# Forgetting attention on one core: low parts of queries against high parts of keys alone, two key chunks at a time on the two halves of the array's rows

## The chip, the cores and the metric

The kernel runs on one core of one Trainium2 chip. The metric is the device time of one launch in microseconds (us). The kernel before took 3076.02 us, the median of three runs (3070.25 to 3080.53).

## The reference

The kernel computes one hybrid layer on 2048 tokens of width 1024 in float32: a norm, one combined input projection, three branches (forgetting attention, a state-space branch with a gated unit, attention into 256 memory tokens), a gated merge, an output projection and a last norm. The change is in the forgetting attention, 12 heads of 64 channels, causal, with a forget term F added to the scores:

```python
def forgetting_attention(q, k, v, log_f):
    F = jnp.cumsum(log_f, axis=1).transpose(0, 2, 1)
    ...
    def block(args):
        qi, Fi, s0 = args
        s = jnp.einsum('bhqd,bhkd->bhqk', qi, kh)
        s = s + Fi[..., None] - F[:, :, None, :]
        qpos = s0 + jnp.arange(Q_BLOCK, dtype=jnp.int32)
        s = jnp.where(key_pos[None, :] <= qpos[:, None], s, NEG)
        p = jax.nn.softmax(s, axis=-1)
        return jnp.einsum('bhqk,bhkd->bhqd', p, vh)
```

## The kernel before

**Numbers in two parts.** Matmuls take operands in a rounded float32 form (float32r). To keep float32 accuracy each operand is split into a high part and a low part, and a product is built from three matmuls: high by high, high by low, low by high (`mm3`, lines 147 to 149).

**Stages.** First come the norm, the transposes and the projections of the four token chunks, with the state-space branch, the gated unit and the memory attention threaded between the projections. Queries, keys and values go to scratch tensors in HBM in high and low parts (`s_qh`, `s_ql`, `s_kh`, `s_kl`, `s_vs`). Then comes the forgetting attention, from about 1605 to 2512 us of the span. A second generator, `fill`, threads the remaining gate projections (`gl`) and part of the merge between its steps, so that TensorE has other work while a softmax is under way. Last come the merge of the other chunks and the output projection.

**The forgetting attention.** `gen_fox` goes through the heads. A head's 16 blocks of 128 queries are taken in eight groups G of two blocks, from the last group to the first, and the short groups alternate with the next head's long ones. A head has 64 channels, and the array has 128 rows, so `fox_keys` (line 706) puts the high parts of 1024 keys in partitions 0 to 63 of the tile `kk` and the low parts in partitions 64 to 127. `fox_q` (line 719) loads the high parts of the queries twice, one copy over the other, as tile `qh`, and the low parts twice as tile `ql`.

`fox_scores` (line 730) takes one block of 128 queries against chunks of 512 keys. A block needs 1 to 4 chunks, by how far back its keys reach; the last chunk may have 128, 256, 384 or 512 keys, and at least 256 columns are computed. Each chunk has a PSUM bank of tag A and two matmuls: line 750 (`qh` with `kk`: high by high plus high by low) and line 751 (`ql` with `kk`: low by high plus low by low). VectorE then adds -F and takes the running maximum out of the bank (line 752), ScalarE takes the exponential (line 757), GpSimd scales the rows (line 761).

`fox_pv` (line 765) follows one group behind. For each two blocks of 128 keys, the rows are transposed by TensorE into a bank of tag B (line 782), ScalarE copies the high part (line 785, or 790 on the diagonal), VectorE takes the low part (line 786 or 791), and line 798 multiplies with the values into the one bank of tag C.

**What sets the order.** The program is built with a scheduler that places the instructions of all the threads in each engine's queue by its own model of time. The eight PSUM banks are divided by tag in the table `PS2` (line 43): A 3, B 3, C 1, F 1. The bank F and, in turn, A serve the threaded projections. All loads of keys and queries are issued by SyncE.

**A place with halves of the array.** The state-space branch already has matmuls that use half of the array, in columns: line 585 multiplies 64 columns of weights at a time into partitions 0 to 63 or 64 to 127 of its bank:

```python
for g in range(2):
    for ri in range(2):
        nc.tensor.matmul(pv[64 * g:64 * g + 64, ri * 256:(ri + 1) * 256],
                         m1t[:, ri * 128 + 64 * g:ri * 128 + 64 * g + 64], u[:, g, :], start=True, stop=True)
```

These are plain float32, and the profile has two records for each. Lines 550, 551 and 572 beside it are transposes and a small matmul of 16 columns.

Of the kernel before, what the change touches and what calls it, by code (L numbers as in the profile page):

```python
# [12 lines left out]
D = 1024  # L13
# [28 lines left out]
PSB = {"A": 2, "B": 3, "C": 2, "F": 1}  # L42
PS2 = {"A": 3, "B": 3, "C": 1, "F": 1}

# [5 lines left out]
class Layer:  # L50
# [83 lines left out]
    def load_w(self, src, shape, pool=None, bufs=2):  # L134
        """One [128, 1024] slab of weights, split into two float32r parts."""
        raw = self.wp.tile([128, 4 * NV], F32, tag="wraw", name="wraw", bufs=2)
        k, m = shape
        n = k * m
        self.nc.sync.dma_start(out=raw[:, :n], in_=src)
        hi, lo = ((pool or self.wp).tile([128, n if bufs == 1 else 1024], F32R, tag=t, name=t, bufs=bufs) for t in ("whi", "wlo"))  # L140
        self.split(hi[:, :n], lo[:, :n], raw[:, :n])
        return (hi[:, :n].rearrange("p (k m) -> p k m", k=k), lo[:, :n].rearrange("p (k m) -> p k m", k=k))

    def mm3(self, out, a, b, first, last):
        """a = (hi, lo) stationary, b = (hi, lo) moving."""
        nc = self.nc
        nc.tensor.matmul(out, a[0], b[0], start=first, stop=False)  # L147
        nc.tensor.matmul(out, a[0], b[1], start=False, stop=False)  # L148
        nc.tensor.matmul(out, a[1], b[0], start=False, stop=last)  # L149

    def rsqrt(self, p, out, ssq, n):
        """out = 1 / sqrt(ssq / D + eps): table square root, then a Newton step."""
        nc = self.nc
        v = p.tile([128, n], F32, tag="nv", name="nv", bufs=2)
        t = p.tile([128, n], F32, tag="nt", name="nt", bufs=2)
        nc.vector.tensor_scalar(out=v, in0=ssq, scalar1=1.0 / D, scalar2=EPS, op0=ALU.mult, op1=ALU.add)
        nc.scalar.activation(t, v, AF.Sqrt)
        nc.vector.reciprocal(out, t)
        nc.vector.tensor_mul(t, out, out)
        nc.vector.tensor_mul(t, t, v)  # L160
        nc.vector.tensor_scalar(out=t, in0=t, scalar1=-0.5, scalar2=1.5, op0=ALU.mult, op1=ALU.add)
        nc.vector.tensor_mul(out, out, t)

    def norm_T(self, src, nt, g, hi, lo, p, xb, split=False):
        """RMSNorm of nt tiles of 128 tokens, then transposed and split: hi, lo [128, KD, nt*128]."""
        nc = self.nc
# [23 lines left out]

# [1 line left out]
    def open_h(self):  # L192
# [63 lines left out]
    def proj_v(self, g, p):  # L256
        """Values of four heads; the forget gates ride with the first four."""
        nc, s = self.nc, self.s
# [29 lines left out]
    def forget(self, p):  # L288
        """-F, the running sum of -log sigmoid(z)."""
        nc, z = self.nc, self.fz  # L290
        e = p.tile([H, L], F32, name="fe")
        nc.vector.scalar_tensor_tensor(out=e, in0=z, scalar=-1.0, in1=z, op0=ALU.mult, op1=ALU.max)
        nc.scalar.activation(e, e, AF.Exp, scale=-1.0)
        nc.scalar.activation(e, e, AF.Ln, bias=1.0)
        nc.vector.scalar_tensor_tensor(out=z, in0=z, scalar=0.0, in1=e, op0=ALU.min, op1=ALU.subtract)
        one = p.tile([H, 1], F32, name="fo")
        nc.vector.memset(one, 1.0)
        nc.vector.tensor_tensor_scan(e, one.to_broadcast([H, L]), z, 0.0, ALU.mult, ALU.subtract)
        nc.sync.dma_start(out=self.s["nf"], in_=e)
# [106 lines left out]

# [1 line left out]
    def s5_exp(self, p, out, x):  # L408
        """exp(x): range reduction by ln 2, polynomial, exact power of two."""
        v = self.nc.vector  # L410
# [14 lines left out]
    def s5_reduce(self, t, n):  # L425
        """t - 2 pi round(t / 2 pi), in place."""
        v = self.nc.vector
# [5 lines left out]
    def s5_sincos(self, p, sn, cs, t, n):  # L433
        """sin and cos of t in [-pi, pi] (t is overwritten) by the quarter angle and two doublings."""
        v = self.nc.vector
# [16 lines left out]
    def cmul(self, outr, outi, ar, ai, br, bi, t):  # L452
        """(outr, outi) = (ar, ai) (br, bi); t is scratch; the outputs are none of the inputs."""
        v = self.nc.vector
# [7 lines left out]
    def s5_prep(self, q, p):  # L462
        """Discretised parameters in the layout [(group parity, state), group pair]; q keeps, p is scratch."""
        nc, v, i = self.nc, self.nc.vector, self.i
# [69 lines left out]
    def s5_pair(self, q, a):  # L534
        """Groups 2a and 2a+1. Chunks of 8 steps: what a chunk adds to the state (M1), the state at each chunk's
        end (a real scan of the states turned back by the phase they have run through), and the outputs from the
        state before the chunk (M2) and from the chunk's own inputs (M3)."""
        nc, v, s = self.nc, self.nc.vector, self.s
# [102 lines left out]

# [1 line left out]
    def mem_scores(self, p, hd, j, b, P):  # L643
# [56 lines left out]

# [1 line left out]
    def open_fox(self):  # L702
# [3 lines left out]
    def fox_keys(self, h, c):  # L706
        """Half a head's keys (high over low parts), values (high beside low) and -F."""
        nc, s, p = self.nc, self.s, self.fp
# [3 lines left out]
        nf = p.tile([128, 1024], F32, tag="nf", name="nf", bufs=3)  # L712
        nc.sync.dma_start(out=fl32(kk[0:64]), in_=s["kh"][r, ks])
        nc.sync.dma_start(out=fl32(kk[64:128]), in_=s["kl"][r, ks])
        nc.sync.dma_start(out=nf, in_=s["nf"][h:h + 1, ks].partition_broadcast(128))
# [14 lines left out]
    def fox_scores(self, p, hd, q, G, P):  # L730
        """Softmax rows of two blocks of 128 queries, the later one first: the mask goes into -F for good, as no
        later block of queries is left to read those keys unmasked."""
        nc = self.nc
        for b in (1, 0):
# [8 lines left out]
            mx = p.tile([128, 4], F32, tag="mx", name="mx", bufs=4)  # L743
            for c in range(nch):
                w = min(512, nk - c * 512)
                wm = max(w, 256)
                kk, _, nf = hd[c // 2]
                c0 = c % 2 * 512
                ps = self.psA()
                nc.tensor.matmul(ps[:, :wm], q[0][:, qs], kk[:, c0:c0 + wm], start=True, stop=False)  # L750
                nc.tensor.matmul(ps[:, :wm], q[1][:, qs], kk[:, c0:c0 + wm], start=False, stop=True)  # L751
                nc.vector.tensor_tensor_reduce(  # L752
                    out=pr[:, c * 512:c * 512 + w], in0=ps[:, :w], in1=nf[:, c0:c0 + w], scale=1.0,
                    scalar=-3.0e38, op0=ALU.add, op1=ALU.max, accum_out=mx[:, c:c + 1])
            nm, den, rd = (p.tile([128, 1], F32, tag=n, name=n, bufs=4) for n in ("nm", "den", "rd"))
# [9 lines left out]
    def fox_pv(self, p, h, hd, G, P):  # L765
        """Columns of the moving operand and of the sums: high parts of the two query blocks, then low parts."""
        nc, s = self.nc, self.s
# [41 lines left out]
    def gen_fox(self):  # L809
        """Heads one after the other, groups of queries from the last to the first; a head's last KS groups, the  # L810
        short ones, alternate with the next head's first ones."""
        p, self.close_f = self.pool("fox", side="right")
# [32 lines left out]

# [1 line left out]
    def gen_glu(self):  # L847
# [39 lines left out]
    def split(self, hi, lo, x, sc=1.0):  # L887
        """sc * x as hi + lo, each exact in float32r."""
        self.nc.gpsimd.tensor_scalar(out=hi, in0=x, scalar1=sc, scalar2=1.0, op0=ALU.mult, op1=ALU.mult)  # L889
# [7 lines left out]
    def ytile(self):  # L897
        """Slots of 4 KB, twelve in the first pool and ten in the second, in the order in which they come free."""
        i, self.ny = self.ny, self.ny + 1
# [20 lines left out]
    def gen_merge0(self):  # L920
        """The last chunk, under the last heads; its share of the attention as soon as the last head is past it."""
        nc, c = self.nc, NC - 1
# [129 lines left out]

# The channels of the state-space branch are kept, 128 at a time, in the order (channel of a group, group).
def host_arrays(x, mem, g_norm, g_mem_norm, g_final, w_in, b_forget, b_merge, w_mem_kv,
# [68 lines left out]
```

## Time and profile before

| | |
|---|---|
| median of three runs | 3076.02 us (3070.25 to 3080.53) |
| span of the profiled execution, first to last instruction | 3072.7 us |
| mean granted TensorE clock | 0.987 |
| PE (TensorE matmul) busy | 2995.7 us |
| DVE (VectorE) busy | 1884.8 us |
| ACT (ScalarE) busy | 927.8 us |
| POOL (GpSimd) busy | 1004.8 us |
| matmuls of lines 750 and 751 | 480 each |

PE is TensorE's matmuls, PEld its weight loads, SP is SyncE. A row of a group gives line, engine, operation, what is written and read, its shape as weights (rows*columns) and output (partitions x columns), the count, the busy time, the mean duration in ns, and then the idle time of the engine just before, with what ended it ("issue" where the profile shows no reason). Matmuls are pipelined: their durations overlap, so that the price of one is read from the distance between two starts. A row of the timeline gives the start, the length to the end of the last one merged into the row, and the count.

### The profile page before, as it was taken

The page shows a single profiled execution, that of the slowest core. Times are in us where ns is not written, and L with a number is a line of the kernel's source. Part 1 is how long each engine was busy: PE and PEld are TensorE (multiplying, and loading weights), DVE is VectorE, ACT ScalarE, POOL GpSimd, SP SyncE. Part 2 cuts the span into 40 slices and gives each one's busy share as a digit, 9 for nine tenths or more (in the row PEclk, how much of TensorE's full clock was granted, in tenths as well). Part 3 has the DMA queues.
Part 4 walks back from the last instruction along what each step waited for, and adds up shares of the span by engine and source line. Part 5 has one row for each costly group of instructions (what it writes and reads, how often), then busy time and mean ns, then how long its engine had stood idle before and what let it go on. Part 6 is the DMA issues. An engine that isn't in the chain of part 4 may idle for free.

```text
span 3072.7 us, 43527 instructions
## 1 busy us (share of the span) xinstructions
PE 2995.7 (97%) x14656; PEld 2438.1 (79%) x14656; DVE 1884.8 (61%) x4982; ACT 927.8 (30%) x1881; POOL 1004.8 (33%) x1328
## 2 busy tenths in 40 slices
PE   9999999999999999999999999999999998999999
PEld 7889977777777778888878888888887786777787
DVE  5333489888886673322217777777777886555544
ACT  5102111111112231222216666666666550000011
POOL 0010000000001332121205665655555766555500
PEclk9999999999999999999999999999999998999999
DMA  5343323323344655344352443544434536665531
GB/s 167 107 136 96 105 84 116 115 84 111 114 132 150 175 164 173 108 127 136 115 165 82 124 121 103 134 121 121 118 111 130 145 108 195 185 182 172 159 108 69
DMA packets 283118, 396.81 MB, mean 129 GB/s; under 512 B 83060, under 2 KB 147828, under 8 KB 282884
## 3 DMA queue, kind: packets, MB, share of 16 engines
q1 hardware_dynamic: 275696, 381.39, 41.8%
q10 hardware_dynamic: 7200, 12.66, 1.2%
q8 instruction: 116, 1.90, 0.3%
q14 instruction: 106, 0.87, 0.1%
HBM read 265.51 MB, written 128.42 MB: 128 GB/s over the span
## 4 chain that ended last, share of the span: by engine, by line
PE 80%; DMA 6%; DVE 5%; issue 4%; POOL 3%; ACT 1%; SPq 0%; DVEq 0%; POOLq 0%; ACTq 0%
PE psF L147 10%; PE psF L148 10%; PE psF L149 10%; PE psA L147 8%; PE psA L148 8%; PE psA L149 8%; PE psC L798 5%; PE psB L782 5%; PE psA L750 3%; PE psA L751 3%; PE psC L147 1%; PE psC L148 1%; PE psC L149 1%; PE psC L585 1%; PE psB L149 1%
## 5 line engine op out<-in xcount | busy, mean ns | idle before, releaser
L147 PE MATMUL psF<-hh,whi 128*128 128x512 f32 (+1 forms) x1160 | 470.2, 405 | 5.3 <-DVE elo L228 2.5
L889 POOL TENSOR_SCALAR whi<-wraw 128x1024 fp32r<-128x1024 f32 (+2 forms) x216 | 204.8, 949 | 795.2 <-PE psA L148 362.0
L149 PE MATMUL psF<-hh,wlo 128*128 128x512 f32 (+1 forms) x1160 | 460.5, 397 | 0.5 <-DVE wlo L891 0.5
L148 PE MATMUL psF<-hl,whi 128*128 128x512 f32 (+1 forms) x1160 | 460.7, 397 | 0.0
L891 DVE TENSOR_TENSOR wlo<-wraw,whi 128x1024 fp32r<-128x1024 f32 (+2 forms) x216 | 260.5, 1207 | 213.4 <-POOL whi L889 189.2
L147 PE MATMUL psA<-hh,whi 128*128 128x512 f32 (+1 forms) x816 | 322.5, 397 | 1.4 <-ACT hh L187 0.8
L148 PE MATMUL psA<-hl,whi 128*128 128x512 f32 (+1 forms) x816 | 322.9, 396 | 0.0
L149 PE MATMUL psA<-hh,wlo 128*128 128x512 f32 (+1 forms) x816 | 321.7, 395 | 0.8 <-DVE wlo L891 0.8
L786 DVE TENSOR_TENSOR Pt<-psB,Pt 128x512 fp32r<-128x512 f32 x336 | 226.2, 685 | 76.3 <-ACT Pt L785 73.9
L798 PE MATMUL psC<-Pt,v 128*128 128x512 f32 x864 | 266.7, 398 | 4.1 <-DVE Pt L786 3.5
L147 PEld LDWEIGHTS psF<-hh,whi 128*128 128x128 f32 x1160 | 219.6, 189 | 52.7 <-DVE elo L228 3.3
L149 PEld LDWEIGHTS psF<-hh,wlo 128*128 128x128 f32 x1160 | 219.5, 189 | 52.0 <-DVE wlo L891 0.9
L148 PEld LDWEIGHTS psF<-hl,whi 128*128 128x128 f32 x1160 | 219.8, 189 | 45.8 <-issue 0.4
L752 DVE CUSTOM_DVE_ANT_0 P<-psA,nf 128x512 f32<-128x512 f32 (+1 forms) x336 | 201.2, 627 | 48.1 <-PE psA L751 28.2
L785 ACT CAST Pt<-psB 128x512 fp32r<-128x512 f32 x336 | 191.9, 586 | 107.4 <-PE psB L782 60.4
L761 POOL TENSOR_SCALAR P<-P,rd 128x768 f32<-128x768 f32 (+1 forms) x240 | 193.2, 821 | 59.6 <-DVE rd L758 36.6
L750 PE MATMUL psA<-kk,qh 128*128 128x512 f32 (+1 forms) x480 | 184.1, 389 | 4.5 <-DVE mx L752 2.6
L147 PEld LDWEIGHTS psA<-hh,whi 128*128 128x128 f32 x816 | 154.1, 189 | 36.9 <-issue 1.6
L149 PEld LDWEIGHTS psA<-hh,wlo 128*128 128x128 f32 x816 | 154.5, 189 | 36.1 <-DVE wlo L891 1.2
L148 PEld LDWEIGHTS psA<-hl,whi 128*128 128x128 f32 x816 | 154.3, 189 | 33.9 <-issue 0.4
L798 PEld LDWEIGHTS psC<-Pt,v 128*128 128x128 f32 x864 | 154.2, 190 | 31.2 <-DVE Pt L786 6.8
L782 PE MATMUL psB<-ident,P 128*128 128x128 f32 x1200 | 177.4, 274 | 0.3 <-POOL P L761 0.2
(343 smaller groups left out, 6228.3 us busy)
## 6 DMA issues: line engine op xcount, KB each, us to landing
wraw<-in_w_in SPq DMA_DIRECT2D x90, 512.0 KB, 4.3
s_gl<-ehi SPq DMA_DIRECT2D x96, 256.0 KB, 2.5
g<-s_gl SPq DMA_DIRECT2D x96, 256.0 KB, 4.6
wraw<-in_w_proj SPq DMA_DIRECT2D x64, 320.0 KB, 2.9
s_vs<-ev_v SPq DMA_DIRECT2D x48, 256.0 KB, 2.7
nf<-s_nf SPq DMA_DIRECT2D x24, 512.0 KB, 6.4
v<-s_vs SPq DMA_DIRECT2D x24, 512.0 KB, 6.4
qh<-s_qh SPq DMA_DIRECT2D x96, 128.0 KB, 3.7
```

The source lines that it names most:

```text
L147: nc.tensor.matmul(out, a[0], b[0], start=first, stop=False)
L148: nc.tensor.matmul(out, a[0], b[1], start=False, stop=False)
L149: nc.tensor.matmul(out, a[1], b[0], start=False, stop=last)
L750: nc.tensor.matmul(ps[:, :wm], q[0][:, qs], kk[:, c0:c0 + wm], start=True, stop=False)
L752: nc.vector.tensor_tensor_reduce(out=pr[:, c * 512:c * 512 + w], in0=ps[:, :w], in1=nf[:, c0:c0 + w], scale=1.0, scalar=-3.0e38, op0=ALU.a ...
L761: nc.gpsimd.tensor_scalar(out=c, in0=c, scalar1=rd, scalar2=0.5, op0=ALU.mult, op1=ALU.mult)
L782: nc.tensor.transpose(ps[:, o:o + 128], P[b][:, kt * 128:(kt + 1) * 128], self.ident)
L785: nc.scalar.copy(hi, psv)
L786: nc.vector.tensor_sub(lo, psv, fl32(hi))
L798: self.pe = nc.tensor.matmul(o, v, m, start=(kt == 0), stop=(kt == 2 * G + 1))
L889: self.nc.gpsimd.tensor_scalar(out=hi, in0=x, scalar1=sc, scalar2=1.0, op0=ALU.mult, op1=ALU.mult)
L891: self.nc.vector.tensor_sub(lo, x, fl32(hi))
```

## The change

The keys' tile is laid out anew: for the even chunk of 512 keys of a tile the high parts stay in partitions 0 to 63 and the low parts in 64 to 127; for the odd chunk it is the other way round. The full matmul with `qh`, which holds the same values in both halves, gives the same sum either way. The low parts of queries are now multiplied, where two chunks stand together, with 64 partitions only, those that hold high parts of keys: 0 to 63 for the even chunk and 64 to 127 for the odd one. The two matmuls use different halves of the array's rows and different banks. The product of low with low parts is left out for these chunks. A chunk without a partner is computed as before, on all 128 rows. A pair's two full matmuls are written first, then its two half ones, then the two reductions on VectorE. The banks of tag A become 4 and those of tag B 2, and each tile of keys comes in four transfers in place of two.

The core of the diff (the rest takes comments and docstrings out and changes nothing that runs; lines of the new file are a few higher, so that the full matmul is line 754, the low one line 760, the transposes line 794 and the matmul with the values line 810):

```diff
-PS2 = {"A": 3, "B": 3, "C": 1, "F": 1}
+PS2 = {"A": 4, "B": 2, "C": 1, "F": 1}
...
-        nc.sync.dma_start(out=fl32(kk[0:64]), in_=s["kh"][r, ks])
-        nc.sync.dma_start(out=fl32(kk[64:128]), in_=s["kl"][r, ks])
+        for a in range(2):
+            cs = slice(c * 1024 + a * 512, c * 1024 + a * 512 + 512)
+            o = slice(a * 512, a * 512 + 512)
+            nc.sync.dma_start(out=fl32(kk[64 * a:64 * a + 64, o]), in_=s["kh"][r, cs])
+            nc.sync.dma_start(out=fl32(kk[64 - 64 * a:128 - 64 * a, o]), in_=s["kl"][r, cs])
...
-            for c in range(nch):
-                w = min(512, nk - c * 512)
-                wm = max(w, 256)
-                kk, _, nf = hd[c // 2]
-                c0 = c % 2 * 512
-                ps = self.psA()
-                nc.tensor.matmul(ps[:, :wm], q[0][:, qs], kk[:, c0:c0 + wm], start=True, stop=False)
-                nc.tensor.matmul(ps[:, :wm], q[1][:, qs], kk[:, c0:c0 + wm], start=False, stop=True)
-                nc.vector.tensor_tensor_reduce(
-                    out=pr[:, c * 512:c * 512 + w], in0=ps[:, :w], in1=nf[:, c0:c0 + w], scale=1.0,
-                    scalar=-3.0e38, op0=ALU.add, op1=ALU.max, accum_out=mx[:, c:c + 1])
+            for c0 in range(0, nch, 2):
+                cs = range(c0, min(c0 + 2, nch))
+                ps = {}
+                for c in cs:
+                    w = max(min(512, nk - c * 512), 256)
+                    o = slice(c % 2 * 512, c % 2 * 512 + w)
+                    ps[c] = self.psA()
+                    full = nc.tensor.matmul(ps[c][:, :w], q[0][:, qs], hd[c // 2][0][:, o], start=True, stop=False)
+                with self.tc.issue_after(full.ins):
+                    for c in cs:
+                        w = max(min(512, nk - c * 512), 256)
+                        o = slice(c % 2 * 512, c % 2 * 512 + w)
+                        hf = slice(64 * (c % 2), 64 * (c % 2) + 64) if len(cs) == 2 else slice(0, 128)
+                        nc.tensor.matmul(ps[c][:, :w], q[1][hf, qs], hd[c // 2][0][hf, o], start=False, stop=True)
+                for c in cs:
+                    w = min(512, nk - c * 512)
+                    o = slice(c % 2 * 512, c % 2 * 512 + w)
+                    nc.vector.tensor_tensor_reduce(
+                        out=pr[:, c * 512:c * 512 + w], in0=ps[c][:, :w], in1=hd[c // 2][2][:, o], scale=1.0,
+                        scalar=-3.0e38, op0=ALU.add, op1=ALU.max, accum_out=mx[:, c:c + 1])
```

The order of TensorE's queue shows it at two places. The first is the start of the forgetting attention, the last block of head 0 with its four chunks. In the kernel before (psA is the chunk's bank, kk the keys, qh and ql the queries):

```order
L750 MATMUL psA_14142<-kk_13057,qh_13071 128x512
L751 MATMUL psA_14142<-kk_13057,ql_13074 128x512
L750 MATMUL psA_14146<-kk_13057,qh_13071 128x512
L751 MATMUL psA_14146<-kk_13057,ql_13074 128x512
L750 MATMUL psA_14150<-kk_13064,qh_13071 128x512
L751 MATMUL psA_14150<-kk_13064,ql_13074 128x512
```

The same block in the changed program:

```order
L754 MATMUL psA_14146<-kk_13057,qh_13075 128x512
L754 MATMUL psA_14148<-kk_13057,qh_13075 128x512
L760 MATMUL psA_14146<-kk_13057,ql_13078 128x512
L760 MATMUL psA_14148<-kk_13057,ql_13078 128x512
L754 MATMUL psA_14154<-kk_13066,qh_13075 128x512
L754 MATMUL psA_14156<-kk_13066,qh_13075 128x512
L760 MATMUL psA_14154<-kk_13066,ql_13078 128x512
L760 MATMUL psA_14156<-kk_13066,ql_13078 128x512
```

What alternated now goes by twos: two full matmuls, then two neighbouring halves on different banks, then again two full ones. The second place is in head 1, a block of three chunks. Before, on TensorE:

```order
L750 MATMUL psA_15473<-kk_14580,qh_15464 128x512
L750 MATMUL psA_15477<-kk_14580,qh_15464 128x512
L750 MATMUL psA_15481<-kk_14851,qh_15464 128x512
L751 MATMUL psA_15473<-kk_14580,ql_15467 128x512
L751 MATMUL psA_15477<-kk_14580,ql_15467 128x512
L751 MATMUL psA_15481<-kk_14851,ql_15467 128x512
```

And in the changed program (psB takes transposes of the softmax rows P, psC the sums with the values v):

```order
L754 MATMUL psA_15481<-kk_14584,qh_15472 128x512
L754 MATMUL psA_15483<-kk_14584,qh_15472 128x512
L754 MATMUL psA_15489<-kk_14857,qh_15472 128x512
L760 MATMUL psA_15481<-kk_14584,ql_15475 128x512
L810 MATMUL psC_15010<-Pt_15068,v_13058 128x2x128
L794 MATMUL psB_15125<-ident_68,P_15024 128x128
L794 MATMUL psB_15125<-ident_68,P_14976 128x128
L794 MATMUL psB_15125<-ident_68,P_15024 128x128
L794 MATMUL psB_15125<-ident_68,P_14976 128x128
L754 MATMUL psA_15510<-kk_14584,qh_15472 128x512
L760 MATMUL psA_15483<-kk_14584,ql_15475 128x512
L760 MATMUL psA_15489<-kk_14857,ql_15475 128x512
```

Here the scheduler has put other work between the two halves of banks 15481 and 15483; the last row is the third chunk's, on all 128 rows. Of the 192 pairs in the program 183 stand as neighbours and 9 are torn apart like this one.

## The prediction

> **What bounds the kernel now.** I read the page first: busy time by engine and, under it, the chain of work that ended last.
>
> ```profile
> PE 2995.7 (97%) x14656; PEld 2438.1 (79%) x14656; DVE 1884.8 (61%) x4982; ACT 927.8 (30%) x1881; POOL 1004.8 (33%) x1328
> PE 80%; DMA 6%; DVE 5%; issue 4%; POOL 3%; ACT 1%; SPq 0%; DVEq 0%; POOLq 0%; ACTq 0%
> ```
>
> TensorE is busy for 97% of a span of 3072.7 us, and 80% of the chain is TensorE. The scores of the forgetting attention run from about 1605 to 2512 us, so next I read the busy times of that stretch alone (columns: stretch, length, then busy us and instructions by engine, clock, DMA share, GB/s), and the groups of instructions in it.
>
> ```profile
> 1605.00:2512.00 907.00, 890.49 (x4770) 739.35 (x4771) 666.05 (x2002) 563.16 (x1127) 548.72 (x784) 0.99 0.42 118
> L750 PE MATMUL psA<-kk,qh 128*128 128x512 f32 (+1 forms) x480 | 184.1, 389 | 4.5 <-DVE mx L752 2.6 <-ACT ehi L238 0.8 <-DMA qh<-s_qh 0.5
> L751 PE MATMUL psA<-kk,ql 128*128 128x512 f32 (+1 forms) x480 | 170.9, 366 | 0.9 <-DMA ql<-s_ql 0.8
> ```
>
> TensorE works 890.5 of these 907 us at a granted clock of 0.99; VectorE, the next, only 666. Its instructions run in the order in which they were written out, so a microsecond of TensorE put in or taken out here moves the end by nearly one. The 389 and 366 ns are durations of overlapping matmuls; the price of one is the distance of starts. The timeline of TensorE (start, length, line) shows it for each width:
>
> ```profile
> 2007.65 0.34 PE L751 MATMUL psA<-kk,ql 128*128 128x384 f32 x1
> 2007.83 0.39 PE L798 MATMUL psC<-Pt,v 128*128 128x512 f32 x1
> ...
> 2010.68 0.40 PE L751 MATMUL psA<-kk,ql 128*128 128x512 f32 x1
> 2010.91 0.39 PE L750 MATMUL psA<-kk,qh 128*128 128x512 f32 x1
> 2011.14 0.39 PE L751 MATMUL psA<-kk,ql 128*128 128x512 f32 x1
> 2011.37 0.28 PE L750 MATMUL psA<-kk,qh 128*128 128x256 f32 x1
> 2011.48 0.28 PE L751 MATMUL psA<-kk,ql 128*128 128x256 f32 x1
> 2011.61 0.40 PE L798 MATMUL psC<-Pt,v 128*128 128x512 f32 x1
> ```
>
> 512 columns cost 0.23 us, 384 cost 0.18 and 256 cost 0.12 (two in 0.24). The weight load of the next matmul lies entirely under the running one.
>
> **What the change takes away.** A head has 16 blocks of queries, four each with one, two, three and four key chunks, hence 16 pairs, 192 over 12 heads. A pair took four matmuls; now it takes two full ones and two half ones that may run at once, so the narrower half disappears. By the order of the changed program 183 pairs stand as two neighbouring halves (111 of 512 with 512 columns, 24 with 384, 48 with 256), and 9 pairs are torn apart into 18 halves that do not stand beside their partner. Saved at most: 111 x 0.23 + 24 x 0.18 + 48 x 0.12 = 25.5 + 4.3 + 5.8 = 35.6 us.
>
> **Does a pair run at once, and what does the switch cost?** No row of the profile has halves of the rows. The nearest are the state-space branch's matmuls of line 585: they use halves of the array's columns (128*64), and lie between full matmuls. Where eight of them alternate between the two halves, and where four stand on one half:
>
> ```profile
> 405.27 1.09 PE L585 MATMUL psC<-u,m1t 128*64 128x256 f32 x8
> 406.29 0.33 PE L551 MATMUL psB<-ident,m1i 128*128 128x128 f32 x1
> ...
> 447.89 0.39 PE L149 MATMUL psF<-hh,wlo 128*128 128x512 f32 x1
> 448.12 0.40 PE L147 MATMUL psF<-hh,whi 128*128 128x512 f32 x1
> 448.45 1.08 PE L585 MATMUL psC<-u,m1t 128*64 128x256 f32 x4
> 449.46 0.61 PE L572 MATMUL psB<-z,bb 128*16 128x128 f32 x4
> ```
>
> Eight took 1.02 us, four 1.01: two halves do run at once, and the second costs nothing, its load included. But the matmul before them, line 147, held the array for 0.33 us instead of 0.23. Entering the mode cost 0.10. The weight loads show why:
>
> ```profile
> 447.89 0.19 PEld L147 LDWEIGHTS psF<-hh,whi 128*128 128x128 f32 x1
> 448.45 0.19 PEld L585 LDWEIGHTS psC<-u,m1t 128*64 128x64 f32 x2 [0.37 <-issue]
> ```
>
> Line 147's load began 0.23 us ahead of its matmul; line 585's began only with it, after an idle of 0.37 us that no semaphore explains. The array empties, and only then is the new load taken. On leaving the same comes again:
>
> ```profile
> 880.57 0.38 PE L585 MATMUL psC<-u,m1t 128*64 128x256 f32 x1
> 880.79 0.38 PE L585 MATMUL psC<-u,m1t 128*64 128x256 f32 x1
> 881.10 0.50 PE L149 MATMUL psF<-hh,wlo 128*128 128x512 f32 x1
> 881.44 0.39 PE L147 MATMUL psF<-hh,whi 128*128 128x512 f32 x1
> 881.67 0.40 PE L148 MATMUL psF<-hl,whi 128*128 128x512 f32 x1
> ```
>
> The pace there is 0.22, but the last half held 0.31 (+0.09), and the first full matmul behind it held 0.34 against 0.23: +0.11 for a load of 128 columns that nothing covers. The half matmuls of the change also load 128 columns, so I take 0.11 on entering too.
>
> In the Trainium skill, "TensorEngine Tiling (Array Packing)", section Key Properties, says that a change of the tiling mode, unlike a change of tile within a mode, drains TensorE. That speaks against this change; these rows agree for halves of columns, 0.10 us, and no run here shows it for halves of rows. The same skill's "TensorE: Matmul & The Clock Gate", section Measured speedup vs the span model, prices a pack of tiles at one matmul and about 4 ns for each further tile, with no term for the switch; by it the sum would stop near the 35.6 us saved.
>
> **The sum.** One set of halves: 0.10 + 0.11 in, 0.09 + 0.11 out, 0.41 us. The order has 183 + 18 = 201 sets, each with full matmuls on both sides. Behind 28 of them comes a transpose, whose uncovered load is cheaper: 451.01 to 451.41 holds a transpose and a matmul in 0.40 us, where 0.11 + 0.23 is usual.
>
> ```profile
> 451.01 0.33 PE L550 MATMUL psB<-ident,m1r 128*128 128x128 f32 x1
> 451.09 0.48 PE L148 MATMUL psF<-hl,whi 128*128 128x512 f32 x1
> 451.41 0.40 PE L149 MATMUL psF<-hh,wlo 128*128 128x512 f32 x1
> ```
>
> So 201 x 0.41 - 28 x 0.05 = 82.4 - 1.4 = 81 us added, 35.6 saved: +45 us. The second half's load is unknown between 0 (line 585, eight in the time of four) and 0.11 behind the first half's; I take 0, and keep 183 x 0.11 = +20 for the range.
>
> The smaller edits I cost at nothing:
> - Banks A from 3 to 4, B from 3 to 2. On A it can win the 2.6 us that line 750 waits for VectorE. On B a transpose (line 782) would wait for its bank's copy and subtraction, 586 + 685 ns, and every later matmul queues behind it.
>
> ```profile
> L786 DVE TENSOR_TENSOR Pt<-psB,Pt 128x512 fp32r<-128x512 f32 x336 | 226.2, 685 | 76.3 <-ACT Pt L785 73.9
> L785 ACT CAST Pt<-psB 128x512 fp32r<-128x512 f32 x336 | 191.9, 586 | 107.4 <-PE psB L782 60.4
> ```
>
>   The stretch has 12 x 36 = 432 such steps, 907 / 432 = 2.1 us each, so 1.3 us of emptying fit beside the work of one step. If that cover failed, I bound it by TensorE's whole idle time there once more, 907 - 890.5 = 16.5 us.
> - The keys come in 96 transfers instead of 48. SyncE spends about 0.55 us on issuing one, so up to 48 x 0.57 = 27 us of 907 on a queue that also issues the queries; TensorE waited 0.5 + 0.8 us for queries (rows above). At most that doubles.
>
> ```profile
> L713 SPq DMA_DIRECT2D kk<-s_kh x24: 445/547/1076, 1550.2 to 2399.3; - x24
> L714 SPq DMA_DIRECT2D kk<-s_kl x24: 584/588/1690, 1550.8 to 2399.8; - x24
> ```
>
> - A pair's first scores reach VectorE some 0.6 us later; it has 907 - 666 = 241 us to spare, and the fourth bank A carries it.
>
> **The rivals.**
> 1. *The switch is free for halves of rows* (0.22). The moving data could go on down the array, and only its lower border change; then nothing empties and nothing is uncovered. For it: two halves of columns do overlap perfectly. Against it: each entry and exit of line 585 pays. It gives 3076.0 - 35.6 = 3040 us, faster. The point from which it decides: 35.6 / 402 = 0.089 us for each of the 402 switches; below that the change wins, and I read 0.20.
> 2. *The array empties, but the load is taken during it* (0.12). 402 x 0.095 = 38.2 against 35.6: +3, 3079 us, no change. Against it: the 0.34 behind line 585.
> 3. *The change does not do what it says: halves of rows take turns* (0.06). Nothing is saved and the switches are paid: +81, 3157 us. Against it: the eight in the time of four.
>
> **How the numbers follow.** The sum belongs to the profiled execution, whose span of 3072.7 us lies 3.3 below the median of the runs, 3076.0 (3070.3 to 3080.5), inside their spread; so I add it to the median. The forecast (0.60): 3076 + 45 = 3121 us, its own range 3105 (a load half covered on one side, 201 x 0.055 = 11, and the banks' gain) to 3142 (second load behind the first). The stated range has to reach rival 1, since both signs hold much: 3039 to 3142 leaves out rival 3 and the outer edges of the others. A measurement of this kernel tells about 0.3%, 9 us, from no change. Faster: rival 1, 0.22. Same: rival 2, 0.12. Slower: 0.60 + 0.06 = 0.66.
>
> **What would show it.** In the changed kernel's timeline: two line-760 matmuls of 64 rows that start within some 20 ns of each other show that halves overlap. The full matmul ahead of them holding about 0.33 us, and the one behind them about 0.34, shows the switch; their weight loads must start late, with idle time put down to issue. TensorE's time for the stretch should grow by about 45 us, with VectorE, ScalarE and GpSimd no busier. The prediction is wrong if full matmuls beside the halves keep 0.23, or if loads of line 760 start 0.2 us ahead of their matmuls. If psB's transposes wait for line 786's successor by more than a few microseconds, the banks were mis-sized.

## The result, and the profile after

The changed kernel takes 3161.2 us (median of four runs, 3160.0 to 3166.9) against 3075.8 (the kernel before, now four runs): it is slower by 85 us, ratio 1.0287, interval 1.0267 to 1.0306. The sign was forecast; the size was not: 3121 us with a range up to 3142.

The busy times on the page after:

```profile
PE 3049.9 (97%) x14656; PEld 2395.0 (76%) x14656; DVE 1885.4 (60%) x4982; ACT 936.2 (30%) x1881; POOL 998.1 (32%) x1328
```

The span is 3159.0 us, 86.3 longer. The other engines do what they did; TensorE is busy for longer, with the same number of matmuls. The forgetting attention, from the first score matmul to the last product with the values, took 931.2 us before and takes 1026.1 now (busy times of the two stretches, before and then after):

```profile
1605.00:2536.20 931.20, 913.48 (x4876) 757.39 (x4877) 685.73 (x2040) 570.99 (x1150) 566.59 (x807) 0.99 0.42 118
```

```profile
1607.50:2633.60 1026.10, 977.70 (x4898) 722.49 (x4899) 690.65 (x2044) 579.34 (x1150) 566.77 (x810) 0.99 0.37 109
```

So 95 us came in here, 2.5 ahead of it, and 11 went out behind it, where the merge now finds more of the threaded work done (TensorE is busy for 490.2 us there, 499.4 before). The idle time of TensorE in the stretch grew from 17.7 to 48.4 us, which no term of the forecast had. First the halves themselves, in TensorE's timeline after:

```profile
2001.41 0.71 PE L754 MATMUL psA<-kk,qh 128*128 128x512 f32 x2
2002.05 0.50 PE L760 MATMUL psA<-kk,ql 64*128 64x512 f32 x2
2002.49 0.68 PE L754 MATMUL psA<-kk,qh 128*128 128x512 f32 x2
2003.09 0.50 PE L760 MATMUL psA<-kk,ql 64*128 64x512 f32 x2
2003.52 0.50 PE L810 MATMUL psC<-Pt,v 128*128 128x512 f32 x1
2003.87 0.27 PE L794 MATMUL psB<-ident,P 128*128 128x128 f32 x1
```

The first set has two halves of 512 columns, the second one of 512 and one of 384. Two halves of 512 columns last 0.50 us from the first start to the second end, not much more than one matmul's 0.39. From the start of a set to the next full matmul pass 0.44 and 0.43 us: an uncovered load of 0.11, one matmul of 0.23 and 0.09 for emptying. Line 810 behind the second set holds 0.35 where 0.23 is the pace. The weight loads of line 760, with the idle time ahead of them:

```profile
L760 PEld LDWEIGHTS psA<-kk,ql 64*128 64x128 f32 (+1 forms) x480 | 56.3, 185 | 64.0 <-issue 60.2 <-DMA ql<-s_ql 2.5
```

60.2 us of idle "issue" over 201 sets is 0.30 us a set: these loads wait for no semaphore that the profile shows, and neither did those of line 585. The prediction's reading of the switch holds for halves of rows.

The other part is waiting. Before, the groups of the transposes and of the product with the values had next to no idle time ahead of them (last columns):

```profile
L798 PE MATMUL psC<-Pt,v 128*128 128x512 f32 x864 | 266.7, 398 | 4.1 <-DVE Pt L786 3.5 <-DVE Pt L791 0.2
L782 PE MATMUL psB<-ident,P 128*128 128x128 f32 x1200 | 177.4, 274 | 0.3 <-POOL P L761 0.2
```

After, TensorE's list of waits (who waited, for whom, us, times, longest) has both:

```profile
PE psB L794 <- DVE Pt L798: 10.6, 15, 1.4
PE psA L754 <- DVE mx L764: 7.1, 12, 1.1
...
PE psC L810 <- DVE Pt L798: 5.9, 11, 1.5
PE psC L810 <- DVE ot L814: 4.6, 4, 1.6
```

Only 10.6 us of this are waits of transposes for a bank B itself. Most of the rest of the list are waits for what comes after a transpose or beside it on VectorE; that they follow from late transposes is not shown wait by wait, but the runs below in which the banks alone differ bring them too. One wait for a bank in the timeline of three engines after:

```profile
2014.22 0.60 PE L794 MATMUL psB<-ident,Ps 128*128 128x128 f32 x4
2014.57 0.37 PE L810 MATMUL psC<-Pt,v 128*128 128x256 f32 x1
2014.78 0.60 PE L794 MATMUL psB<-ident,Ps 128*128 128x128 f32 x4
2014.91 0.59 ACT L797 CAST Pt<-psB 128x512 fp32r<-128x512 f32 x1 [1.38 <-PE psB L794]
...
2015.53 0.69 DVE L798 TENSOR_TENSOR Pt<-psB,Pt 128x512 fp32r<-128x512 f32 x1 [1.25 <-ACT Pt L797]
...
2016.37 0.52 PE L794 MATMUL psB<-ident,Ps 128*128 128x128 f32 x3 [0.99 <-DVE Pt L798]
```

Two sets of transposes start 0.56 us apart and fill both banks B. The third must wait until the first bank has been copied (0.59 us) and subtracted (0.69 us), and TensorE, with all later matmuls queued behind it, stands idle for 0.99 us.

I added up all distances between starts in the stretch, matmul by matmul. What a distance has beyond the pace of its width is booked as a switch term at its usual size (entering 0.095; a set of halves up to the next matmul 0.430 in place of its last half's own pace; the first load behind 0.107; a neighbouring half 3 ns after the first in place of its own pace) or, if over 0.1 us remains, as a wait (a few lost records count there too, in all kernels alike).

| | switch terms, us | waits, us |
|---|---|---|
| before | 0 | 35 |
| after | 19 + 47 + 20 - 42 = +44 | 79 |

Forty-four of switches (forecast: 45) and forty-four more of waits (forecast: none); about 5 us of threaded work that moved into the stretch and small remainders make up the rest of the 95.

### The profile page after: what moved, and what is told of

It is laid out like the page before. It is cut to its first block, busy times and chain, and to the rows that moved or that the text cites. A ratio compares the mean times of both kernels' runs of the same rounds, so it can differ in the third digit from the quotient of the medians.

```text
span 3159.0 us, 43657 instructions
## 1 busy us (share of the span) xinstructions
PE 3049.9 (97%) x14656; PEld 2395.0 (76%) x14656; DVE 1885.4 (60%) x4982; ACT 936.2 (30%) x1881; POOL 998.1 (32%) x1328
## 4 chain that ended last, share of the span: by engine, by line
PE 79%; DVE 6%; DMA 6%; issue 4%; POOL 3%; ACT 2%; SPq 0%; DVEq 0%; POOLq 0%; ACTq 0%
PE psF L147 10%; PE psF L148 10%; PE psF L149 10%; PE psA L147 8%; PE psA L149 8%; PE psA L148 8%; PE psC L810 5%; PE psB L794 5%; PE psA L754 3%; PE psA L760 2%; PE psC L148 2%; PE psC L149 2%; PE psC L147 2%; PE psC L585 1%; DVE P L764 1%
## 5 line engine op out<-in xcount | busy, mean ns | idle before, releaser
L810 PE MATMUL psC<-Pt,v 128*128 128x512 f32 x864 | 280.7, 407 | 15.2 <-DVE Pt L798 5.9
L741 POOL TENSOR_TENSOR nf<-nf,mask 128x128 f32<-128x128 f32 x192 | 94.4, 495 | 287.6 <-DVE mx L764 232.1
```

Source lines behind the costliest of these rows:

```text
L810: self.pe = nc.tensor.matmul(o, v, m, start=(kt == 0), stop=(kt == 2 * G + 1))
```

## The experiments

Theory 1: two costs, the switch for halves and the missing third bank B. Rival 2: everything is the halves. Rival 3: what comes beyond the switch is the order full, full, half, half. The four kernels of the first group were timed beside a kernel before of 3073.0 us. Where kernels of different groups are compared below, two numbers are given: the difference of what each lost against the kernel before beside it, and the difference of the two medians.

**Banks put back.** The changed kernel with `PS2 = {"A": 3, "B": 3, ...}`.

> The changed kernel with the banks as they were (A 3, B 3). In its order 179 pairs stand as neighbours and 26 halves alone, 205 sets. Theory 1 (two costs: each set of halves pays for emptying the array and for uncovered loads, about +50 us in all, and the two banks B make the transposes and the products with the values wait for VectorE, about +35 us): the second cost goes, some 3125 us, the switches stay. Rival 2 (all of the 85 us belongs to the halves, which take turns or pay more at a switch than was read): 3160 us, as the changed kernel. Rival 3 (the extra 35 us come from the order full, full, half, half, which hands VectorE its scores later): 3160 us as well.

Measured 3113.0 us, ratio 1.0127 (1.0111 to 1.0144): 40 us slower than before, 45 to 48 faster than the change. Rivals 2 and 3 fall. The same account of its trace gives switch terms of 20 + 47 + 21 - 41 = +47 us and waits of 28, 7 less than before, and its list of waits has for the transposes only this:

```profile
PE psB L794 <- DVE Pt L798: 0.5, 1, 0.5
```

This is the kernel that the prediction had in fact worked out, with +45.

**Banks alone.** The kernel before with `PS2 = {"A": 4, "B": 2, ...}`.

> The kernel before with only the banks of the change (A 4, B 2), no halves, keys laid out as before. Theory 1: the transposes wait for banks B here too; about +25 to +35 us, 3100 to 3111 us. Rivals 2 and 3: nothing in it costs, 3076 us.

Measured 3161.8 us, ratio 1.0285 (1.0265 to 1.0304): +89, as slow as the whole change. Theory 1 has the right cause and a size some three times too small. By the same account the waits in its stretch are 121 us. So the two costs don't add: 89 and 40 alone, 85 together.

**No halves.** In the changed kernel, all low matmuls on all rows:

```diff
-hf = slice(64 * (c % 2), 64 * (c % 2) + 64) if len(cs) == 2 else slice(0, 128)
+hf = slice(0, 128)
```

> The changed kernel with all low matmuls on all 128 rows, so that low parts meet low parts too as in the kernel before; pairing, key layout, transfers and banks of the change stay, and the order of TensorE's queue hardly differs from the changed kernel's. Theory 1: the price of the halves goes (about 50 us), the waits stay: about 3111 us. Rival 2: all of it goes, 3076 us. Rival 3: like theory 1, 3111 us; it differs from theory 1 in the run with the banks put back.

Measured 3141.8 us, ratio 1.0225 (1.0209 to 1.0240), 31 more than theory 1 had. With these banks the halves add only 17 to 19 us (3161 against 3142): the account shows waits of 98 us here and 79 with the halves. I read it so, and no run shows it by itself: time that TensorE loses in a switch is time in which banks B are emptied, so that a later wait is shorter by it. The rival of this section that blames the order is turned round by this run: with the order, key layout and transfers of the change it is 20 us faster than the banks alone, which keep the old ones. TensorE's waits for queries on their way in, 4.8 us here and 18.9 there by their lists of waits, are the larger part of that.

**Lone halves.** The kernel before, with the low matmul of the first chunk of each pair on rows 0 to 63:

```diff
-kk, _, nf = hd[c // 2]
+(kk, _, nf), hf = hd[c // 2], slice(0, 64 if c % 2 == 0 and c + 1 < nch else 128)
...
-nc.tensor.matmul(ps[:, :wm], q[1][:, qs], kk[:, c0:c0 + wm], start=False, stop=True)
+nc.tensor.matmul(ps[:, :wm], q[1][hf, qs], kk[hf, c0:c0 + wm], start=False, stop=True)
```

> The kernel before, its key layout, banks and order of TensorE's queue kept, but in each pair of chunks the even chunk's low matmul stands on rows 0 to 63 alone (high parts of keys), the odd one's on all rows. 192 lone halves with nothing beside them: this measures the switch by itself. Theory 1, with the changed kernel's trace: per half 0.095 + 0.107 + 0.231 + 0.095 + 0.107 against 0.231 us, 0.40 more; 192 of them, 30 with a transpose behind: about +76 us, 3152 us. If the cost of a pair is that its halves take turns and the switch is free, nothing is lost here: 3076 us.

Measured 3131.7 us, ratio 1.0193 (1.0174 to 1.0213): +59. The switch is not free, and not shared with anything here. TensorE's timeline of one of them:

```profile
1886.07 0.40 PE L149 MATMUL psF<-hh,wlo 128*128 128x512 f32 x1
1886.30 0.40 PE L750 MATMUL psA<-kk,qh 128*128 128x512 f32 x1
1886.63 0.49 PE L751 MATMUL psA<-kk,ql 64*128 64x512 f32 x1
1887.06 0.50 PE L750 MATMUL psA<-kk,qh 128*128 128x512 f32 x1
1887.39 0.40 PE L751 MATMUL psA<-kk,ql 128*128 128x512 f32 x1
```

0.33, 0.43 and 0.33 us where 0.23 stood three times: 0.40 more, as read from line 585. The account books 18 + 38 + 19 = 75 us of switches, which is the 76 expected, and waits that fall from 35 to 19: 16 of the 17 us that are missing.

The second group asks which number of the banks matters and why (kernel before beside it: 3072.3 us).

**Two banks B, one bank idle.** The kernel before with `PS2 = {"A": 3, "B": 2, ...}`.

> The kernel before with A 3 and B 2, so that one of the eight banks lies idle. The banks of the change alone cost 89 us; which of the two numbers did it? If it is the third bank B that is missing: about 3160 us or a little more, since the fourth bank A is missing too. If it is the division A 4 to B 2 as a whole, or chance in what the scheduler makes of it: near 3073 to 3100 us.

Measured 3152.7 us, ratio 1.0264 (1.0247 to 1.0280): +80. The third bank B is the cause. That A 4, B 2 is slower still by 9 us is not explained. Nor are the waits only for bank B itself: in this trace TensorE also waits 18.2 us for queries on their way in, where it waited 1.3 before (its list of waits here):

```profile
PE psA L750 <- DMA qh<-s_qh: 9.3, 8, 4.4
PE psA L751 <- DMA ql<-s_ql: 8.9, 10, 1.5
```

What sets off those is open; the changed kernel has 2.2 us of them for `qh` and 0.6 for `ql`.

**Bank B free after the copy, by a subtraction within SBUF.** The kernel before, once with A 4, B 2 and once with A 3, B 3, with this edit at lines 786 and 791 (the low parts become zero):

```diff
-nc.vector.tensor_sub(lo, psv, fl32(hi))
+nc.vector.tensor_sub(lo, fl32(hi), fl32(hi))
```

> The kernel before with A 4 and B 2, and with the low part of the transposed rows taken as high minus high, so that it is zero and VectorE no longer reads bank B: the bank is free after ScalarE's copy (about 0.59 us) and not after copy and subtraction (about 1.27 us). The low parts of the softmax rows are left out. If the time that a bank B is held is the cause, most of the 89 us goes: within 30 us of the same edit with A 3, B 3. If the cause is the order made for these banks or VectorE's queue, 60 to 90 us stay.

> The control for the run above: the same edit (low parts of the softmax rows left out, bank B free after the copy) with A 3, B 3. Both theories: about as the kernel before, 3060 to 3075 us.

Measured 3151.7 us (ratio 1.0263, 1.0241 to 1.0285) with two banks and 3118.0 us (1.0149, 1.0132 to 1.0166) with three. The control missed by over 40 us, so this pair decides little. The control's groups of instructions show what else the edit changed:

```profile
L786 DVE TENSOR_TENSOR Pt<-Pt 128x512 fp32r<-128x512 f32 x336 | 325.0, 983 | 32.7 <-ACT Pt L785 32.1
...
L761 POOL TENSOR_SCALAR P<-P,rd 128x768 f32<-128x768 f32 (+1 forms) x240 | 244.2, 1032 | 74.9 <-DVE rd L758 55.4 <-PE psC L798 8.8 <-PE psA L751 7.2
```

With its operands in SBUF the subtraction took 983 ns in place of 685, and GpSimd's scaling slowed from 821 to 1032 at the same time. The order of TensorE's queue is another too, and what part of the control's 46 us each has is open. Still, a bank less cost 34 us here and 80 to 89 without the edit.

**Both halves on the same rows.** The changed kernel with A 3, B 3, the keys laid out as before, and

```diff
-hf = slice(64 * (c % 2), 64 * (c % 2) + 64) if len(cs) == 2 else slice(0, 128)
+hf = slice(0, 64) if len(cs) == 2 else slice(0, 128)
```

> The changed kernel with A 3, B 3 (3113 us), but the keys laid out as before and both half matmuls of a pair on rows 0 to 63, so that they can't run at once; sets of halves and switches stay. If halves on different rows really overlap, as their starts 3 ns apart say, this loses 111 x 0.23 + 24 x 0.18 + 48 x 0.12 = 35.6 us: about 3148 us. If they only seem to overlap in the records, 3113 us.

Measured 3140.7 us, ratio 1.0227 (1.0201 to 1.0253): 28 more than with halves on different rows (3113.0, in the other group). TensorE's timeline of a pair:

```profile
2015.43 0.47 PE L754 MATMUL psA<-kk,qh 128*128 128x512 f32 x1
2015.83 0.73 PE L760 MATMUL psA<-kk,ql 64*128 64x512 f32 x2
2016.49 0.50 PE L754 MATMUL psA<-kk,qh 128*128 128x512 f32 x1
```

0.66 us from the pair to the next, where halves on different rows need 0.43: they take turns here, by 0.23, and don't there. The prediction's rival 3, whose 3157 us lie so near the result, is refuted.

The third group (kernel before: 3073.3 us) has the clean test of the banks and a test of the number of switches.

**The subtraction reads the spare bank.** The kernel before with A 3, B 2; the eighth bank (a tag Z of its own) holds zeros, and VectorE reads it at lines 786 and 791 in place of bank B, so that this kernel leaves out the right low parts of the softmax rows:

```diff
-nc.vector.tensor_sub(lo, psv, fl32(hi))
+nc.vector.tensor_sub(lo, self.z, fl32(hi))
```

> The kernel before with A 3 and B 2 (3153 us), the eighth bank filled with zeros; VectorE's subtraction reads that bank in place of bank B, so that it is as long as before but bank B is free after ScalarE's copy. The low parts of the softmax rows are wrong values in this run. If the time that a bank B is held is the cause of the 80 us: below 3100 us. If the cause lies elsewhere (the order for two banks, the length of the chain from transposes to the product with the values): 3130 us and more.

Measured 3074.3 us, ratio 1.0001 (0.9990 to 1.0011): the whole 80 us are gone. Here the control holds, for the operation's group has its old duration:

```profile
L786 DVE TENSOR_TENSOR Pt<-psZ,Pt 128x512 fp32r<-128x512 f32 x336 | 227.4, 686 | 72.1 <-ACT Pt L785 69.8
L785 ACT CAST Pt<-psB 128x512 fp32r<-128x512 f32 x336 | 192.5, 583 | 131.7 <-PE psB L782 90.1 <-PE psC L798 39.9 <-DVE Pt L786 0.5
```

In this kernel two banks B suffice, with each held until the copy is done and not until the subtraction is. The scheduler, which knows of the earlier release, also laid out another order; what part of the 80 us is the order, and what the release itself, is open. The pair before also released bank B after the copy and still lost 34 us to the missing bank, beside a longer subtraction.

**Two banks A, four banks B.** The kernel before with `PS2 = {"A": 2, "B": 4, ...}`.

> The kernel before with A 2 and B 4. If banks B are what counts, this is no slower than the kernel before and perhaps faster by up to 15 us of waits (3058 to 3076 us), unless two banks A make the scores wait in turn: then 3090 us and more.

Measured 3096.3 us, ratio 1.0062 (1.0043 to 1.0082): +23, in the second of the two expected ranges: the scores wait in turn, for line 750 waits 8.6 us for VectorE to empty its bank A, where it waited 2.6 before. A fourth bank B wins nothing that makes up for a third bank A.

**One set for a block of four chunks.** The changed kernel with its own banks, chunks taken four at a time:

```diff
-for c0 in range(0, nch, 2):
-    cs = range(c0, min(c0 + 2, nch))
+for c0 in range(0, nch, 4):
+    cs = range(c0, min(c0 + 4, nch))
...
-hf = slice(64 * (c % 2), 64 * (c % 2) + 64) if len(cs) == 2 else slice(0, 128)
+hf = slice(64 * (c % 2), 64 * (c % 2) + 64) if c // 2 * 2 + 2 <= nch else slice(0, 128)
```

> The changed kernel with its banks (A 4, B 2), but a block of four chunks issues its four full matmuls first and then its four halves, alternating between the halves of the rows: 144 sets instead of 201, none torn apart. If each set costs about 0.40 us, as the changed kernel's trace adds up, 57 sets fewer and 9 pairs more save about 25 us: 3136 us. If the sets cost little beside the waits for banks B, or if four banks A held at once bring waits of their own: 3161 us or more.

Measured 3140.5 us, ratio 1.0211 (1.0193 to 1.0229): 18 to 21 less than the change, near the 25 expected. Fewer switches for the same pairs pay 0.32 to 0.36 us each (18 / 57 and 21 / 57, the repaired pairs included). No version came out faster than the kernel before, and by these prices none of this kind is in sight that could be measured. A set with two pairs of 512 columns saves 0.46 us and costs 0.40, and only 12 blocks of four chunks have two such pairs: 12 x 0.06 = 0.7 us, an estimate from these rows.

## Why the prediction was right and wrong

- *A set of halves costs 0.41 us, 201 sets.* Right. The rows of line 760 show 0.33 for the full matmul ahead, 0.43 or 0.44 for the set and 0.34 or 0.35 behind; the account books 44 us net where the sum had 45, and the run with the banks put back came out 40 slower. Reading the price of halves of rows from halves of columns was sound here.
- *The second half is free, its load included; 0 taken, +20 kept.* Right: the second start comes 3 ns after the first, whatever the width, and the run with both halves on the same rows lost 28 us.
- *"Banks A from 3 to 4, B from 3 to 2" cost nothing, at most 16.5 us.* This step failed, and it makes the miss of 40 us. Alone it costs 89 us; in the changed kernel the account has 44 us more of waits than before. The cover was put as 1.3 us of emptying beside 2.1 us of work a step. Both numbers misled. 2.1 us is a mean: at 2014.22 and 2014.78 two steps stand 0.56 us apart with no threaded work between them. And 1.3 us is copy and subtraction alone, without the time that a filled bank waits for either engine. At the first transposes before, three banks are filled in 1.53 us (12 transposes), and the last of the three subtractions ends at 1629.15:

```profile
1624.95 1.53 PE L782 MATMUL psB<-ident,P 128*128 128x128 f32 x12 [0.18 <-POOL P L761]
...
1626.18 1.54 ACT L785 CAST Pt<-psB 128x512 fp32r<-128x512 f32 x3
...
1627.27 1.88 DVE L786 TENSOR_TENSOR Pt<-psB,Pt 128x512 fp32r<-128x512 f32 x3
```

  Counted filling by filling in that trace, a bank B is taken for 3.7 us in the median and 4.1 in the mean, from its first transpose to the end of its subtraction; with two banks each comes round every 2 x 2.1 = 4.2 us, which leaves nothing over. In 191 of the 432 steps the transposes start before the subtraction of the filling two ahead has ended: there the third bank was the cover. (In the changed kernel this is so in 20 steps, all behind a filling of the diagonal, which is emptied in two parts.) With two banks in the changed kernel the copy starts 0.09 us behind its transposes in the median, where it was 1.0: the transposes no longer run ahead. The bound was wrong too: idle time under three banks says nothing of what a third bank keeps away. The prediction's own sign of this, transposes that wait for the subtraction by more than a few microseconds, came with the 10.6 us.
- *The sum in one piece.* Switches and waits were taken as terms that add. They overlap on TensorE: with two banks B the halves add 17 to 19 us instead of 40.
- *VectorE, ScalarE and GpSimd no busier; keys' transfers hidden.* Right: 685.7 and 690.7 us of VectorE in the stretch. TensorE's matmuls waited 2.2 and 0.6 us for queries, where 0.5 and 0.8, at most doubled, were forecast.
- *Rival 3 (3157 us).* Its number was met by accident; its mechanism is refuted.
- *The range.* Its lower end does not add up: 3121 less 11 and less 2.6 is 3107, not 3105. The miss is at the other end, where the range had no term for the banks.

## What to carry to other kernels

Halves of the array pay only if many of them stand together: read the price of going in and out from any matmul of another tile shape in the same trace (here 0.40 us a set), and hold it against what one pair saves (here 0.23 us at most). When a change also moves PSUM banks, cost that edit by itself, and not with mean work per step: count in the trace before how long a filling lies in its bank, waits included, and how often the next filling but one begins earlier. If one edit makes the bounding engine slower and another makes it wait, they can overlap, as here, and cost less than their sum.

## What the runs showed of the hardware

- A set of matmuls on 64 rows paid for emptying what line 585's on 64 columns did, 0.095 us on entry and again on exit, and each time 0.107 us for a load of 128 columns that nothing covered. The Trainium skill, "TensorEngine Tiling (Array Packing)", section Key Properties, says that a change of mode drains TensorE; the runs agree and add the uncovered load, which is the larger part.
- Two half matmuls on different rows, into different banks, start 3 ns apart and last as long as a lone one (0.50 and 0.49 us), in float32r and with 128 columns of weights each. On the same rows the second starts 0.34 us after the first.
- VectorE's subtraction was slower with its operands in SBUF (983 ns) than with one in PSUM (685 ns), and GpSimd slowed beside it (1032 against 821 ns). The Trainium skill, "GPSIMD Engine Reference", section Specifications, says that GpSimd shares its SBUF interfaces with VectorE and contends with VectorE's instructions that have two SBUF inputs. The trace agrees: where the second operand was a PSUM bank, the spare one, the subtraction was back at 686 ns. No run here takes GpSimd away to show it by itself.
